# Head of a two-layer hybrid diffusion step: norm by halves, adaLN by quarters, gate tiles moved, merges split by chunks

## The chip, the cores and the metric

The kernel runs on one core of a Trainium2 chip. The metric is the device time of one launch in microseconds (us), lower is better; the time given is the median of several runs. The engines are TensorE (PE in the profile, PEld for its weight loads), VectorE (DVE), ScalarE (ACT), GpSimd (POOL) and SyncE (SP, which here only issues DMAs). Each works through its own instructions in order and waits on semaphores.

## The reference

Two layers (D = 1024 channels) run over a context of 128 tokens and a latent grid of 512 tokens, which share all weights. What matters here:

```
mod = silu(c) @ w_mod[l] + b_mod[l]              # adaLN: 6 x 1024 values, one row for context, one for latent
sh1, sc1, g1, sh2, sc2, g2 = split(mod, 6)
h = rmsnorm(x, norm1_g) * (1 + sc1) + sh1
proj = h @ w_in                                   # qkv, z, beta/alpha, hyena, fourier, three gates
merged = sigmoid(gate_a) * (y_a @ w_pa) + sigmoid(gate_b) * (y_b @ w_pb) + sigmoid(gate_c) * (y_c @ w_pc)
x = x + g1 * (merged @ w_o)
h = rmsnorm(x, norm2_g) * (1 + sc2) + sh2
x = x + g2 * ((silu(h @ w_g) * (h @ w_u)) @ w_down)
```

y_a is a chunked gated DeltaNet with scans in both directions, y_b a Hyena convolution of order 2 (its filters come from a small MLP with sines), y_c a Fourier mixing. A position table is added to the latent tokens first, and a last rmsnorm closes the trunk.

## The kernel before

Activations lie channels by tokens, as 8 tiles (k) of 128 channels by 640 tokens, worked on in two chunks (c) of 320 tokens. The products keep about fp32 accuracy with three matmuls: operands are split in a rounded hi part and a remainder lo, and out = hi*hi + hi*lo + lo*hi. `split` makes the pair: ScalarE writes hi, POOL (or VectorE) subtracts for lo. A weight of 128x1024 (512 KB) comes by SP into `wr` (two buffers) and is split into `wh` and `wl` (four buffers of 512 columns), in the order of `_stream` (line 50).

A planner written in Python (lines 360 to 495) decides at build time how the work is interleaved. Each engine has an estimated clock; the main line of `mixer` and `ffn` emits matmuls, and after every six of them calls `pump`, which lets generators in the background (`bg`) emit a step when their estimated due time has come. A step's `yield hint` says how early it may run. `finish` emits what is left of a generator at once. On the chip each engine then keeps the emitted order.

*Head* (`run`, line 2116). The filter MLP, `embed` (position table, squares of x, then `rstd`), `cond` (the conditioning vector) and `mods` for adaLN tiles 0 to 15 run as generators in the planner's order; the norm starts when `embed` and `mods` are done. `mods` (line 699) takes four tiles (a group) at a time: 32-column matmuls with the weights streaming, ScalarE copies the row, a turn through TensorE brings it into columns, VectorE adds the bias. `norm` (line 807) multiplies x by the reciprocal norm, then scales and shifts with `mod`, and splits into h. It needs sh1 (groups 0 and 4) and sc1 (groups 8 and 12). `mixer` then asks with `need` for all eight tiles of a chunk before it emits the small beta/alpha projection and the qkv projections. x is written to DRAM (`xS`) before the mixer and read back before the output projection.

*adaLN later on.* All other groups come through one tile S: each half of a group (K halves, 1024 KB) is loaded, waited for, multiplied, and only then the next half is loaded. The planner's due time grows by 4.0 us per step, beside the load's estimate. Groups 28 to 40 (layer 0) and 32 to 40 (layer 1) run beside the scans' last batch, and `self.finish(*gd, *gm)` (line 1891) closes both.

*After the scans* (line 1892 on): `delta_out` norms and gates the scans' output in the background while two tiles of gate c are projected; `finish(go)`; then the Fourier branch (`fnet`) and behind it `hyena` start in the background; four merges of branch a (two channel tiles each); four of branch c, with the gate tiles 2 to 7 between; eight gate tiles of branch b; `finish(gh)`; four merges of branch b. The last merge of a tile scales it by 0.5 and splits it, over all 640 tokens. The output projection reads the eight split tiles in order of k, chunk 0 first.

Sizes of tiles in the profile's names: `A` is a large tile, `T` 640 tokens, `U` 512 columns, `pg` and `ps` PSUM banks (three and five).

Of the kernel before, what the change touches and what calls it, by code (L numbers as in the profile page):

```python
# [18 lines left out]
P = 128  # L19
# [30 lines left out]
def _stream():  # L50
    s = [("ba", 0)] + [("in", m * P) for m in QKV_ORDER]
    s += [("in", OFF_FN + m * P) for m in range(4)]
    s += [("in", 1536 + m * P) for m in range(4)]
    s += [("in", OFF_HY + m * P) for m in range(12)]
    gate = lambda br, m: ("in", OFF_G + BR[br] * D + m * P)
    s += [gate("a", m) for m in range(8)]
    s += [gate("c", 0), gate("c", 1)]
    s += [("pa", m) for m in range(0, 8, 2)]
    s.append(("pc", 0))
    for m in range(2, 8, 2):  # L60
# [243 lines left out]
class _Net:  # L304
# [377 lines left out]
    def cond(self):  # L682

        nc = self.nc
        ct = self.kp.tile([P, 2 * KD + 30], F32, name="ct")
        nc.vector.memset(ct[:, 2 * KD:], 0.0)
        nc.sync.dma_start(ct[:, :2 * KD], self.I["cT"])
        nc.sync.dma_start(self.small, self.I["small"])
        nc.scalar.activation(ct[:, :2 * KD], ct[:, :2 * KD], AF.Silu)
        self.ct = [ct[:, 2 * k:2 * k + 32] for k in range(KD)]  # L690
# [8 lines left out]
    def mods(self, l, lo, hi, par=False, hint=0.5, first=False):  # L699

# [17 lines left out]

        def add(ps, w, h):
            for k in range(KD // 2):  # L720
                for g in range(4):
                    nc.tensor.matmul(ps[32 * g:32 * g + 32, :P], self.ct[4 * h + k], w[g][:, k * P:k * P + P],
                                     start=h + k == 0, stop=h == 1 and k == 3)

        W = {}
        if first:
            for j in range(lo, hi, 2):
                S = self.A()
                for i in range(2):
                    if j + i == hi - 4:  # L730
# [5 lines left out]
        for j in range(lo, hi, 4):  # L736
            ps = None
            for h in range(2):
                if first:
                    w = [W[j + g][:, h * 512:h * 512 + 512] for g in range(4)]  # L740
                else:
                    w = [S[:, g * 512:g * 512 + 512] for g in range(4)]
                    nc.sync.dma_start(S[:, :2048].rearrange("p (g c) -> p g c", g=4),
                                      self.I["wmod"][l, j:j + 4, :, h * 512:h * 512 + 512].rearrange("g p c -> p g c"))
# [4 lines left out]
                if first and j == lo and not h:  # L749
                    self.tables()  # L750
# [7 lines left out]
            last = j, row  # L758
        self.on(last[1])
        yield hint  # L760
        turn(*last)
# [15 lines left out]
    def rstd(self, u, n, w):  # L777

        nc = self.nc
        if u == 0:  # L780
            self.rb = []
# [3 lines left out]
        for t in range(n):  # L785
            nc.tensor.matmul(ps[:w, t:t + 1], self.ssq[:, u + t * w:u + t * w + w], self.ones[:, 0:1],
                             start=True, stop=True)
        m = self.p2.tile([P, 5], F32, tag="nm", name=self.nm("nm"))[:w, :n]
# [18 lines left out]
    def norm(self, l, gcol, sh, scl, new, place, alt=False):  # L807
# [5 lines left out]
        for s in range(2):  # L813
            v.scalar_tensor_tensor(out=a[:, s], in0=mv[:, s, scl:scl + KD], scalar=1.0,
                                   in1=par[:, gcol:gcol + KD], op0=ALU.add, op1=ALU.mult)
# [7 lines left out]
        for c in range(2):  # L823
            yield from self.wait(c)
            new(c)
            for k in range(2):
                head(k, c)
            for k in range(KD):
                t, hi, lo = q.pop(0)
                for s, u, w in (((0, 0, TP), (1, TP, NC)), ((1, 0, NC),))[c]:  # L830
                    x, g, b = t[:, u:w], a[:, s, k:k + 1], mv[:, s, sh + k:sh + k + 1]
                    if alt and k % 2:
# [3 lines left out]
                if k + 2 < KD:  # L836
# [11 lines left out]
    def norm_mod(self, l, gcol, sh, scl, alt=False):  # L848
        def new(c):
# [6 lines left out]
            y[:, c * NC:(c + 1) * NC] for y in self.h[k]]), alt)  # L856
# [61 lines left out]
    def filters(self, l):  # L918
# [30 lines left out]
        for sl in (slice(0, TS), slice(TS, T)):  # L949
# [4 lines left out]
            yield  # L954
            ps = self.ps()
# [6 lines left out]
            nc.vector.tensor_tensor(out=hs[64:, sl], in0=h2[64:, :n], in1=th[64:, :n].bitcast(F32), op=ALU.subtract)  # L962
            yield
        if not l:
            self.pre = True
# [818 lines left out]
    def merge(self, br, m, th, first, last):  # L1784
# [3 lines left out]
        for i in range(2):  # L1788
            mt = self.mg[(m + i) // 4][:, (m + i) % 4]
            for c in range(2):  # L1790
# [4 lines left out]
                if not first:  # L1795
                    nc.vector.tensor_tensor(out=mt[:, sl], in0=mt[:, sl], in1=th[i][:, sl], op=ALU.add)
                self.pump()
# [13 lines left out]
    def mixer(self, l, co):  # L1811
# [82 lines left out]
        for m in range(2):  # L1894
# [11 lines left out]
        for m in range(0, 8, 2):  # L1906
            if m:
# [3 lines left out]
            else:  # L1911
                self.finish(gf)
            self.merge("c", m, th, False, False)
# [19 lines left out]
        g = self.mod[l][:, :, 16:24]  # L1933
        self.lots(2 * (KD - O_SPLIT))
# [159 lines left out]
    def embed(self):  # L2094
# [7 lines left out]
        for k in range(KD):  # L2102
# [6 lines left out]
            if k:  # L2109
                self.sq_add(k - 1)  # L2110
            yield
        self.sq_add(KD - 1)
        yield
        yield from self.rstd(0, 5, P)

    def run(self):
# [5 lines left out]
        self.step(self.ff)  # L2122
        self.x = self.x_tile()
        n = self.bg(self.embed())
        self.step(n)
        self.cond()
        m = self.bg(self.mods(0, 0, MODS0, first=True))
        self.step(m)
        while not (n.done and m.done):
            self.finish_one([co for co in (n, m, self.ff) if not co.done])  # L2130
            if m.t > 30.0 and not self.nunit:
                self.free(0, 0)
        self.gm = self.bg(self.mods(0, MODS0, MODS1))
        self.pre = False
        self.rs, self.hn = [n, n], 0
        self.co = self.bg(self.norm_mod(0, C_G1, 0, 8, True))
        for l in range(self.depth):
            for i in range(2):
                nc.sync.dma_start(self.xS[:, 4 * i:4 * i + 4], self.xA[i])
# [100 lines left out]
```

## Time and profile before

| | |
|---|---|
| median of 3 runs | 2749.7 us (2746.98 to 2753.47) |
| the profiled execution's own time | 2748.93 us |
| its span, first to last instruction | 2747.2 us |
| TensorE busy | 2542.1 us, 93% |
| VectorE, ScalarE, POOL busy | 1784.8, 1101.5, 1272.3 us |
| mean granted TensorE clock | 0.963 |

Times in the rows are us from the span's start. A granted clock of 1.00 is 2.4 GHz, of 0.50 1.2 GHz; a stretch with both has a value between. Matmul ends are modelled, so a busy TensorE is not TensorE at its peak. A bracket behind a row says how long the engine sat idle before it and what released it. All instructions go through one helper, so they have one line number; the tiles' names tell them apart.

### The profile page before, as it was taken

The page shows a single profiled execution, that of the slowest core. Times are in us where ns is not written, and L with a number is a line of the kernel's source. Part 1 is how long each engine was busy: PE and PEld are TensorE (multiplying, and loading weights), DVE is VectorE, ACT ScalarE, POOL GpSimd, SP SyncE. Part 2 cuts the span into 40 slices and gives each one's busy share as a digit, 9 for nine tenths or more (in the row PEclk, how much of TensorE's full clock was granted, in tenths as well). Part 3 has the DMA queues.
Part 4 walks back from the last instruction along what each step waited for, and adds up shares of the span by engine and source line. Part 5 has one row for each costly group of instructions (what it writes and reads, how often), then busy time and mean ns, then how long its engine had stood idle before and what let it go on. Part 6 is the DMA issues. An engine that isn't in the chain of part 4 may idle for free. (4 is left out here: it accounts for less than half of the span.)

```text
span 2747.2 us, 55957 instructions
## 1 busy us (share of the span) xinstructions
PE 2542.1 (93%) x22520; PEld 2411.4 (88%) x22520; DVE 1784.8 (65%) x3375; ACT 1101.5 (40%) x2383; POOL 1272.3 (46%) x1228
## 2 busy tenths in 40 slices
PE   5897999979999999999988989889999999999998
PEld 3786988979999999999977779778889998999997
DVE  5467977444645686667665789665456358777775
ACT  4454464422332343333335544534223333444442
POOL 2334325332335576666632352333333365776662
PEclk8998999989999999999989999989999999999999
DMA  7442663534554235422222437425255441222222
GB/s 295 171 164 63 162 146 90 155 134 146 204 191 169 62 128 173 162 78 85 85 97 90 144 79 184 115 65 159 95 200 193 163 167 47 85 85 77 85 76 79
DMA packets 125683, 353.57 MB, mean 129 GB/s; under 512 B 11994, under 2 KB 26330, under 8 KB 118944
## 3 DMA queue, kind: packets, MB, share of 16 engines
q1 hardware_dynamic: 107856, 312.76, 34.2%
q0 software_dynamic: 17568, 37.24, 7.1%
q8 instruction: 177, 2.90, 0.4%
q14 instruction: 82, 0.67, 0.1%
HBM read 288.60 MB, written 37.24 MB: 119 GB/s over the span
## 5 line engine op out<-in xcount | busy, mean ns | idle before, releaser
L2189 PE MATMUL pg<-A,wh 128*128 128x320 f32 (+1 forms) x6304 | 1456.0, 318 | 44.3 <-POOL A L2189 10.4
L2189 PEld LDWEIGHTS pg<-A,wh 128*128 128x128 f32 (+1 forms) x6304 | 1070.5, 192 | 87.0 <-POOL A L2189 18.0
L2189 PE MATMUL pg<-A,wl 128*128 128x320 f32 (+1 forms) x3152 | 990.5, 314 | 2.3 <-DMA wl<-wr 1.8
L2189 POOL TENSOR_TENSOR wl<-wr,wh 128x512 fp32r<-128x512 f32 (+2 forms) x374 | 524.3, 1415 | 513.8 <-ACT wh L2189 486.4
L2189 PEld LDWEIGHTS pg<-A,wl 128*128 128x128 f32 (+1 forms) x3152 | 603.5, 191 | 7.1 <-DMA wl<-wr 4.2
L2189 ACT CAST wh<-wr 128x512 fp32r<-128x512 f32 (+2 forms) x486 | 287.0, 609 | 278.8 <-PE pg L2189 231.4
L2189 PE MATMUL ps<-A,wh 128*128 128x320 f32 x1696 | 378.8, 310 | 0.0
L2189 PEld LDWEIGHTS ps<-A,wh 128*128 128x128 f32 x1696 | 283.9, 188 | 1.4 <-issue 1.0
L2189 PE MATMUL ps<-A,wl 128*128 128x320 f32 x848 | 263.5, 311 | 5.0 <-POOL wl L2189 4.8
L2189 POOL TENSOR_TENSOR wl<-U,wh 128x512 fp32r<-128x512 f32 x160 | 227.8, 1441 | 43.5 <-ACT wh L2189 43.5
L2189 POOL DMA_DIRECT2D wl<-wr x112 | 98.7, 912 | 277.7 <-ACT wl L2189 264.6
L2189 PE MATMUL ps<-A,A 32*32 32x32 f32 (+5 forms) x2984 | 205.3, 239 | 9.3 <-DVE A L2189 5.5
L2189 PEld LDWEIGHTS ps<-A,A 32*32 32x32 f32 (+2 forms) x2984 | 177.3, 142 | 20.2 <-DVE A L2189 6.0
L2189 DVE TENSOR_TENSOR T<-T,T 128x320 f32<-128x320 f32 (+1 forms) x139 | 133.6, 961 | 83.7 <-ACT T L2189 79.4
L2189 POOL TENSOR_TENSOR A<-A,A 128x640 fp32r<-128x640 f32 (+5 forms) x84 | 122.2, 1473 | 121.0 <-ACT A L2189 113.1
L2189 DVE TENSOR_TENSOR A<-A 128x120 f32<-128x120 f32 (+23 forms) x690 | 161.0, 297 | 14.0 <-DMA A<-hyS 10.8
L2189 PEld LDWEIGHTS ps<-A,wl 128*128 128x128 f32 x848 | 159.7, 188 | 7.4 <-POOL wl L2189 7.3
L2189 ACT CAST wh<-U 128x512 fp32r<-128x512 f32 x160 | 99.2, 621 | 165.4 <-PE ps L2189 60.0
L2189 PE MATMUL pg<-A,A 128*128 128x320 f32 x1056 | 161.0, 310 | 0.0
L2189 PEld LDWEIGHTS pg<-A,A 128*128 128x128 f32 x1056 | 156.3, 188 | 0.7 <-issue 0.2
L2189 DVE STREAM_TRANSPOSE A<-A 32x1024 f32<-32x1024 f32 x72 | 151.2, 2120 | 1.5
L2189 DVE TENSOR_TENSOR U<-ps,U 128x512 f32<-128x512 f32 x144 | 77.9, 542 | 103.3 <-PE ps L2189 66.8
(165 smaller groups left out, 3194.7 us busy)
## 6 DMA issues: line engine op xcount, KB each, us to landing
wr<-in_wbig_dram SPq DMA_DIRECT2D x272, 512.0 KB, 3.7
A<-in_wmod_dram SPq DMA_DIRECT2D x40, 1024.0 KB, 6.4
A<-hT SPq DMA_DIRECT2D x32, 1024.0 KB, 7.7
wl<-wr POOLq DMA_DIRECT2D x112, 256.0 KB, 4.5
kSp<-U SPq DMA_DIRECT2D x40, 256.0 KB, 2.0
U<-kSp SPq DMA_DIRECT2D x40, 256.0 KB, 8.7
A<-in_wmod_dram SPq DMA_DIRECT2D x16, 512.0 KB, 10.2
hyS<-T SPq DMA_DIRECT2D x24, 320.5 KB, 3.1
```

The lines of the kernel that those rows point to most:

```text
L2189: return f(*a, **k)
```

## The change

It has four parts and some moves that belong to them.

- *Head.* The order of the generators' steps is written out by hand. adaLN groups come in the order 0, 8, 4, 12 (loads and matmuls), each turned at once. `norm` gets `halves`: channels 0 to 511 of chunk 0, then of chunk 1, then channels 512 to 1023 of each; the gain is computed per half. The first half needs groups 0 and 8 only. `embed` emits its adds and squares without yields between. `mixer` of layer 0 asks for 12 of 16 tiles before chunk 0 instead of 8. The write of x to `xS` moves behind the small projection of chunk 0. In the filter MLP both first layers come before both second ones, and its last subtraction goes from VectorE to POOL.
- *adaLN later on.* Quarters of K (512 KB) into two alternating halves of S, each load issued one step ahead of its use. The 4.0 us are added per quarter.
- *Gate c.* Four of its tiles, not two, stand between `finish(*gd, *gm)` and `finish(go)`; the merges c of tiles 0 and 2 then follow each other. The order of the weights follows.
- *Merged branches.* The split of the last merge goes per chunk of 320 tokens, for the last two tiles with VectorE; the factor 0.5 is multiplied once into the gate g1.

```diff
@@ _stream
-    s += [gate("c", 0), gate("c", 1)]
+    s += [gate("c", m) for m in range(4)]
@@ mods
+        nq = 2 if first else 4
+        w1 = D // nq
...
+            js = js[::2] + js[1::2]
...
+            todo = [(j, h) for j in range(lo, hi, 4) for h in range(nq)]
+
+            def load():
+                j, h = todo.pop(0)
+                w = S[:, h % 2 * D:h % 2 * D + D]
+                nc.sync.dma_start(w.rearrange("p (g c) -> p g c", g=4),
+                                  self.I["wmod"][l, j:j + 4, :, h * w1:h * w1 + w1].rearrange("g p c -> p g c"))
+
+            load()
+        for j in js:
             ps = None
-            for h in range(2):
+            for h in range(nq):
...
+                    w = [S[:, h % 2 * D + g * w1:h % 2 * D + g * w1 + w1] for g in range(4)]
+                    if todo:
+                        load()
                 self.on(*w, *([last[1]] if last else []))
                 if not first:
                     self.cur.t += 4.0
                 yield hint
@@ norm
-        for c in range(2):
+        for k0, c in ((k0, c) for k0 in range(0, KD, n) for c in range(2)):
             yield from self.wait(c)
-            new(c)
-            for k in range(2):
+            if k0 == 0:
+                new(c)
+            if halves and c == 0:
+                gain(k0, n)
+            for k in range(k0, k0 + 2):
                 head(k, c)
-            for k in range(KD):
+            for k in range(k0, k0 + n):
@@ merge
+                if last:
+                    hi, lo = [x[(m + i) // 4][:, (m + i) % 4][:, sl] for x in self.mgs]
+                    self.split(hi, lo, mt[:, sl], nc.vector if m == 6 else None)
                 self.pump()
-            if last:
-                hi, lo = self.mgs[0][(m + i) // 4][:, (m + i) % 4], self.mgs[1][(m + i) // 4][:, (m + i) % 4]
-                nc.vector.tensor_scalar(out=mt, in0=mt, scalar1=0.5, scalar2=None, op0=ALU.mult)
-                self.split(hi, lo, mt)
@@ mixer
-            self.need(c * KD + KD)
+            self.need(c * KD + KD if l or c else KD + KD // 2)
...
+            if c == 0:
+                for i in range(2):
+                    nc.sync.dma_start(self.xS[:, 4 * i:4 * i + 4], self.xA[i])
...
-        for m in range(2):
+        for m in range(4):
             th.append(self.Tt())
             self.gate(l, "c", m, th[m])
...
-            if m:
+            if m == 0:
+                self.finish(gf)
+            if m > 2:
                 th = [self.Tt() for _ in range(2)]
...
+        nc.vector.tensor_scalar(out=g, in0=g, scalar1=0.5, scalar2=None, op0=ALU.mult)
@@ run
+        for x in (m, cd, ff, n, ff, m, m, n, n, ff, m, m, n, *[co] * 4, m, m):
+            self.step(x)
+        self.free(0, 0)
+        for x in (*[co] * 4, ff):
+            self.step(x)
+        while not m.done:
+            self.step(m)
```

In `run`, `m` is `mods`, `cd` `cond`, `ff` the filters, `n` `embed`, `co` the norm.

## Rows read from the trace of the kernel before

**Rows 1.** The page: the span, and busy time of each engine with its share and instructions.

```profile
span 2747.2 us, 55957 instructions
...
PE 2542.1 (93%) x22520; PEld 2411.4 (88%) x22520; DVE 1784.8 (65%) x3375; ACT 1101.5 (40%) x2383; POOL 1272.3 (46%) x1228
```

**Rows 2.** Timeline of the head: start, us, engine, line, operation, tiles, [idle before].

```profile
9.92 0.69 DVE L2189 TENSOR_TENSOR A<-A,U 128x512 f32<-128x512 f32 x1 [4.96 <-DMA A<-in_xT_dram]
...
22.10 2.14 DVE L2189 SCALAR_TENSOR_TENSOR U<-U,U 128x512 f32<-128x512 f32 x3
...
31.23 12.77 SPq L2189 DMA_DIRECT2D xS<-A  x2
...
44.51 0.83 DVE L2189 TENSOR_TENSOR T<-T,T 128x640 f32<-128x640 f32 x1
...
44.69 0.59 PE L2189 MATMUL ps<-small,U 128*128 128x8 f32 x2 [4.82 <-ACT U L2189]
...
52.41 0.89 DVE L2189 TENSOR_TENSOR U<-A,ps 128x320 f32<-128x320 f32 x2 [1.43 <-PE ps L2189]
...
57.69 0.87 POOL L2189 TENSOR_TENSOR A<-U,A 128x320 fp32r<-128x320 f32 x1 [0.26 <-ACT A L2189]
...
63.00 0.46 PE L2189 MATMUL pg<-A,wh 128*128 128x320 f32 x2
...
76.86 0.33 PE L2189 MATMUL pg<-A,wh 128*32 128x320 f32 x1 [0.61 <-POOL A L2189]
```

**Rows 3.** Busy time by stretch: us, each engine, granted clock, DMA share, GB/s.

```profile
54.00:63.00 9.00, 6.90 (x24) 2.76 (x25) 8.61 (x20) 8.20 (x19) 5.47 (x7) 0.65 0.67 252
63.00:79.00 16.00, 15.39 (x129) 13.66 (x128) 4.29 (x9) 10.53 (x28) 11.34 (x11) 1.00 0.25 67
```

**Rows 4.** Timeline, scans' end of layer 0, and one row of layer 1.

```profile
539.51 1.08 PE L2189 MATMUL ps<-A,ct 128*32 128x128 f32 x32
...
549.02 1.08 PE L2189 MATMUL ps<-A,ct 128*32 128x128 f32 x32
...
550.17 9.26 SPq L2189 DMA_DIRECT2D A<-in_wmod_dram  x2
...
557.08 1.93 PE L2189 MATMUL ps<-A,ct 128*32 128x128 f32 x32 [5.00 <-DMA A<-in_wmod_dram]
...
564.10 1.94 PE L2189 MATMUL ps<-A,ct 128*32 128x128 f32 x32 [4.57 <-DMA A<-in_wmod_dram]
...
566.32 2.71 ACT L2189 ACTIVATE U<-A 128x512 f32<-128x512 f32 x5
...
582.76 3.84 DVE L2189 TENSOR_TENSOR A<-A,A 128x640 fp32r<-128x640 f32 x2 [1.42 <-ACT A L2189]
...
1916.52 1.08 PE L2189 MATMUL ps<-A,ct 128*32 128x128 f32 x32
```

**Rows 5.** Timeline, TensorE inside the merges of branch a.

```profile
602.55 0.56 PE L2189 MATMUL pg<-A,wh 128*128 128x320 f32 x2 [4.34 <-DVE A L2189]
```

**Rows 6.** Timeline, last merges to output projection, layer 0.

```profile
872.26 1.46 DVE L2189 TENSOR_SCALAR A<-A 128x640 f32<-128x640 f32 x1
...
874.53 0.41 PE L2189 MATMUL pg<-A,wh 128*128 128x320 f32 x1 [1.49 <-ACT A L2189]
...
876.15 0.63 PE L2189 MATMUL pg<-A,wh 128*128 128x320 f32 x1 [1.20 <-POOL A L2189]
```

**Rows 7.** DMA issues of the page: how many, KB each, median us to landing.

```profile
wr<-in_wbig_dram SPq DMA_DIRECT2D x272, 512.0 KB, 3.7
A<-in_wmod_dram SPq DMA_DIRECT2D x40, 1024.0 KB, 6.4
```

**Rows 8.** Timeline, 48 projection matmuls in a row, as a gate tile has.

```profile
66.53 7.19 PE L2189 MATMUL pg<-A,A 128*128 128x320 f32 x48
```

**Rows 9.** Timeline, VectorE before the last merges of layer 0.

```profile
839.73 0.49 DVE L2189 SCALAR_TENSOR_TENSOR A<-A,pg 128x320 f32<-128x320 f32 x1 [26.59 <-PE pg L2189]
```

More of the change, by code (lines that the diff above doesn't have):

```diff
@@ L56, in _stream @@
     s += [gate("a", m) for m in range(8)]
-    s += [gate("c", 0), gate("c", 1)]
+    s += [gate("c", m) for m in range(4)]
     s += [("pa", m) for m in range(0, 8, 2)]
-    s.append(("pc", 0))
-    for m in range(2, 8, 2):
+    s += [("pc", 0), ("pc", 2)]
+    for m in range(4, 8, 2):
         s += [gate("c", m), gate("c", m + 1), ("pc", m)]
@@ L687, in cond @@
         nc.sync.dma_start(ct[:, :2 * KD], self.I["cT"])
-        nc.sync.dma_start(self.small, self.I["small"])
+        self.ct = [ct[:, 2 * k:2 * k + 32] for k in range(KD)]
+        yield
         nc.scalar.activation(ct[:, :2 * KD], ct[:, :2 * KD], AF.Silu)
-        self.ct = [ct[:, 2 * k:2 * k + 32] for k in range(KD)]
     def tables(self):
@@ L757, in mods @@
             nc.scalar.copy(row, ps[:, :P])
[L758 to L761, printed above, removed]
+            if first:
+                turn(j, row)
+            else:
+                last = j, row
+        if last:
+            self.on(last[1])
+            yield hint
+            turn(*last)
     def sq_add(self, k, c=None):
@@ L787, in rstd, with spread @@
                              start=True, stop=True)
+        yield from self.spread(ps, u, n, w)
+    def spread(self, ps, u, n, w):
+        nc = self.nc
+        if u == 0:
+            self.rb = []
         m = self.p2.tile([P, 5], F32, tag="nm", name=self.nm("nm"))[:w, :n]
@@ L805, in wait, with norm @@
             yield lambda: self.rs[c].t if len(self.rs) > c and self.rs[c].done else None
-    def norm(self, l, gcol, sh, scl, new, place, alt=False):
+    def norm(self, l, gcol, sh, scl, new, place, halves=False):
         nc = self.nc
@@ L812, in norm, with gain @@
         a = self.p2.tile([P, 2, KD], F32, tag="na", name=self.nm("na"))
-        for s in range(2):
-            v.scalar_tensor_tensor(out=a[:, s], in0=mv[:, s, scl:scl + KD], scalar=1.0,
-                                   in1=par[:, gcol:gcol + KD], op0=ALU.add, op1=ALU.mult)
+        def gain(u, n):
+            for s in range(2):
+                v.scalar_tensor_tensor(out=a[:, s, u:u + n], in0=mv[:, s, scl + u:scl + u + n], scalar=1.0,
+                                       in1=par[:, gcol + u:gcol + u + n], op0=ALU.add, op1=ALU.mult)
+        if not halves:
+            gain(0, KD)
+        n = KD // 2 if halves else KD
         q = []
@@ L831, in norm @@
                     x, g, b = t[:, u:w], a[:, s, k:k + 1], mv[:, s, sh + k:sh + k + 1]
-                    if alt and k % 2:
+                    if halves and k % 2:
                         nc.scalar.activation(x, x, AF.Identity, bias=b, scale=g)
@@ L855, in norm_mod @@
         return self.norm(l, gcol, sh, scl, new, lambda k, c: (self.U()[:, :NC], *[
-            y[:, c * NC:(c + 1) * NC] for y in self.h[k]]), alt)
+            y[:, c * NC:(c + 1) * NC] for y in self.h[k]]), halves)
     def norm_blocks(self, l, gcol, sh, scl):
@@ L954, in filters @@
             yield
+        for sl in (slice(0, TS), slice(TS, T)):
+            n = sl.stop - sl.start
             ps = self.ps()
@@ L1910, in mixer @@
                     self.gate(l, "c", m + i, th[i])
-            else:
-                self.finish(gf)
-            self.merge("c", m, th, False, False)
+            self.merge("c", m, th[:2], False, False)
+            del th[:2]
         self.y["c"] = None
@@ L2122, in run @@
         self.step(self.ff)
+        cd = self.bg(self.cond())
+        self.step(cd)
         self.x = self.x_tile()
@@ L2125, in run @@
         self.step(n)
-        self.cond()
+        nc.sync.dma_start(self.small, I["small"])
         m = self.bg(self.mods(0, 0, MODS0, first=True))
[L2128 to L2132, printed above, removed]
+        self.rs, self.hn = [n, n], 0
+        co = self.co = self.bg(self.norm_mod(0, C_G1, 0, 8, True))
+        ff = self.ff
+        for x in (m, cd, ff, n, ff, m, m, n, n, ff, m, m, n, *[co] * 4, m, m):
[5 more added lines that the diff above has]
+            self.step(m)
+        assert n.done and self.hn == 8
         self.gm = self.bg(self.mods(0, MODS0, MODS1))
         self.pre = False
-        self.rs, self.hn = [n, n], 0
-        self.co = self.bg(self.norm_mod(0, C_G1, 0, 8, True))
         for l in range(self.depth):
-            for i in range(2):
-                nc.sync.dma_start(self.xS[:, 4 * i:4 * i + 4], self.xA[i])
             self.mixer(l, self.co)
```

36 lines of the change are left out of this document (15 added, 21 removed).

## The prediction

> **What bounds the kernel now.** I read the page first: TensorE is busy 2542.1 of the 2747.2 us span [rows 1]. The change removes no matmul, so what it can win is TensorE's idle time, some 200 us, and the time that TensorE spends at its lower clock after such idling. So I then listed TensorE's waits in order of time, with what ended each, and for each edit looked up the wait that it is aimed at. Four places matter.
>
> *The head.* The first 128x128 projection starts at 63.00 us [rows 2]. Until then TensorE works in scraps. VectorE adds the position table to x and sums the squares; the last sum ends at 45.34, behind it the last adaLN turn (44.69), and the first multiply of the norm comes at 52.41 [rows 2]. Lo of the norm's fourth tile is done at 58.56 [rows 2]: four tiles take 6.15 us. Between 54 and 63 us the granted clock is 0.65, a mixture of 1.2 and 2.4 GHz, and VectorE is busy 8.61 of 9.00 us; between 63 and 79 us it is 1.00 and TensorE is full [rows 3].
>
> *The end of the scans in layer 0.* Four of the six adaLN half tiles have run by 550.1. The last two each wait for their load, 5.00 and 4.57 us, in a clock that has meanwhile fallen (32 matmuls take 1.94 us in place of 1.08) [rows 4]. Their issue holds SP's queue for 9.26 us. ScalarE can only begin the scans' output at 566.32, and that output ends at 586.60 on VectorE [rows 4]. In layer 1 the last half tile ran at 1916.52 without such a wait [rows 4]: there the main stream still had matmuls left.
>
> *Inside the merges of branch a*, TensorE waits 4.34 us for VectorE, which at that moment prepares the Fourier branch and so returns no PSUM bank [rows 5].
>
> *Between the last merges and the output projection.* After the last merge VectorE scales a 128x640 tile by 0.5 (1.46 us), ScalarE rounds it, POOL subtracts; TensorE waits 1.49 and then 1.20 us [rows 6]. The same pair stands once more in layer 1 (1.47 and 1.20): two layers, one pattern.
>
> **The change part by part.** *Norm by halves (head).* The norm of channels 0 to 511 needs only the adaLN groups 0 and 8, which are now loaded and computed first; groups 4 and 12 are needed for the second half. The work does not shrink, so I follow the new hand-written order along its in-order queues, with durations of before. VectorE: one sine chain (three operations of 2.14 us in all [rows 2], with the two scalings and the clamp some 3.5), then 8 position adds of 0.69 and 7 sums of 0.83, 11.3 us, from when the first half of x lands at 9.92 [rows 2]: squares summed at about 22, not 45.3. From the last turn to the norm's first multiply before took 52.41 - 45.28 = 7.1 us. The new order puts more in front: the first group's turn behind a small sine (together 3), the second long sine on VectorE (3.5), on ScalarE its sine and two copies (1.9), and only behind those the copy and turn of group 8 (1.0). 22 + 3 + 7.1 + 3.5 + 1.9 + 1.0 = 38.5 for the first multiply, not 52.41. Then the halves stand one after the other, each behind an adaLN turn that waits for ScalarE: chunk 0 until POOL gets its fourth tile, 57.69 - 52.41 = 5.3 [rows 2]; turn 1.1; chunk 1, which has one piece per tile and not two, an estimated four fifths of that, 4.2; the small second sine with its ScalarE steps, estimated a little under the long one's, 3.2; turn and gain 1.6; that is 53.9. The second half of chunk 0 takes the same 6.15 us as four tiles before, and the matmuls behind it 0.9: the projection starts at 61.0, not 63.00. So of 14 us won at the norm's start 2.0 reach TensorE. Chunk 1 before also waited in its small projection (0.61 in the row shown [rows 2], some 0.9 over it); now it is ready long before. Sum: 2.9 us gained. Bounds: 8 gained, if the turns do not hold the halves apart; 1 lost, if the scraps keep the clock at 1.2 GHz until 64.
>
> The write of x to DRAM, which held SP from 31.23 for 12.77 us [rows 2] while it waited for the last add, goes behind the first small projection. SP is then free for weights; the same 2.6 MB move later, beside a TensorE that is full and a DMA share of 0.25 [rows 3]: nothing either way. The two hyena subtractions that go from VectorE to POOL lie where POOL has nothing to do: nothing.
>
> *adaLN by quarters.* 40 loads of 1024 KB become 80 of 512 KB into two alternating halves of the tile, each issued one step ahead; the matmuls are the same. The planner adds 4 us to a step, now per quarter. Before, a half tile came every 9.4 us (540.59 to 550.10 [rows 4]); a quarter can come no sooner than 4 us plus its 16 matmuls, and pumps are 6 matmuls, 0.9 us, apart [rows 8], so I take 5.5. From the first, near 519, seven of twelve quarters fit before the scans end at 552.08 [rows 4] and five are left, not two halves of six. A 512 KB load lands in 3.7 us where a 1024 KB one takes 6.4 [rows 7]. Two quarters are there already or on their way; behind them two pairs of load and matmuls of some 4.3 us each: the turn ends near 563, not 566.9 (564.10 + 1.94 + 0.9 for copy and turn). Gain 4 us. Layer 1, by the same pace: three of eight quarters left where one half was; the end moves from 1918.5 to about 1920.2: 1.7 us lost. Sum 2.3 gained. Bounds: 13.8 gained, if the quarters keep up and the wait goes altogether (15 us from 552 to 567, less 3.7 of work, and 2.5 for gate tiles that no longer run at 1.2 GHz); 4 lost, if two quarters more are left in each layer. The other adaLN stretches lie beside a full TensorE, with nobody waiting for their loads: nothing.
>
> A rule speaks against this edit: the Trainium skill (DMA: Bandwidth & Descriptors, Bandwidth) asks for transfers of 1 MiB or more, since each pays a fixed part; its section Anatomy of one DMA gives 2.0 us plus bytes at 436 KB/us, an estimate of 3.2 us for a quarter and 4.4 for a half. By that two quarters cost 2.0 us more than a half wherever they don't overlap; by the trace it is 2 x 3.7 - 6.4 = 1.0 [rows 7], the same direction. With 3.2 for 3.7 the two pairs above would end 1 us sooner, 3.3 us gained by this edit in place of 2.3.
>
> *Four tiles of gate c ahead of the scans' output.* A gate tile is 48 matmuls, 7.19 us [rows 8]. Two more now cover the scans' output; but that output ended at 586.60, just as the merges of branch a began, with no wait between [rows 4], so in the old order there is nothing to win. The 4.34 us inside the merges [rows 5] stay: the Fourier branch still starts behind the scans' output and lands in the same merges. What pays is the hyena branch, which loses 14.4 us of matmuls beside it. VectorE is idle for 26.59 us before 839.73, hyena being done [rows 9], so 12 us of cover remain. I take 0; bounds 3 gained (a shorter wait at the Fourier branch's end) and 4 lost (two merges in a row beside hyena's first round, both on VectorE).
>
> *Merged branches by chunks.* The 0.5 moves into the residual gate (one tiny operation for eight of 1.46 us), the rounding runs per 320 columns, the last two tiles subtract on VectorE. The output projection reaches the last tile 21 matmuls, 3.1 us, after its start, and chunk 0 of it is then complete. Both waits go: 1.49 + 1.20, in two layers 5.4 us. Bounds 6 and 2 (ScalarE's sixteen short copies for eight long ones).
>
> **Sum**: 2.9 + 2.3 + 0 + 5.4 = 10.6 us. From the profiled execution's 2748.9 (span 2747.2 and 1.7 around it; the median shown is 0.8 higher) that gives 2738.3; I say 2738.
>
> **Rivals.** *Much faster*: the quarters end with the scans and TensorE never falls to 1.2 GHz there. For it: both loads would be one step ahead. Against it: the 4 us per step. 2.9 + 13.8 + 5.4 = 22.1 us, 2727; with the head at its bound, 2722. *No change*: quarters pace worse than halves (seven left in layer 0, five in layer 1: 4 lost), the head gives 0 because TensorE enters the projection at 1.2 GHz, and the last merges give 5: about 2748. For it: the head's clock of 0.65 [rows 3], and that two loads of 512 KB take 1.0 us more than one of 1024 KB [rows 7]. The rule of the Trainium skill named above (DMA: Bandwidth & Descriptors) points to this rival. *Slower*: the hyena branch outlasts gates b. It decides from 12 us on, and each us beyond is paid in both layers; to end 5.5 us above before it must outlast by 8.1, so its 160 us must grow by some 20. For it: two merges in a row add VectorE work to its first round. Against it: later rounds lose the same work. At 10 us over, 2758. *The change doesn't do what it says*: gate c covers nothing, as costed; that is inside the forecast.
>
> **How the numbers follow.** Forecast (3 to 20 us faster) 0.54; much faster 0.22; no change 0.14; slower 0.10. A difference under 0.2% (5.5 us) is about what a measurement of this kernel cannot tell from none: above 2744.2 the forecast's small end counts as no change. Faster 0.74, same 0.17, slower 0.09. The forecast's own range is 2730 to 2745; with the much-faster case and half of the no-change case, 2720 to 2749.
>
> **What would show it.** Head: first norm multiply near 38, first 128x128 projection near 61. If the projection starts before 56, ScalarE's turns didn't hold it; if after 63, the hand-written order did. Scans' end: two waits of adaLN matmuls for loads of some 3 us each in layer 0, last turn near 563. Output projection: no wait behind the last merges. Merges of branch a: a wait of about 4 us for VectorE, still there. Gates b: VectorE idle some 12 us before the last merges; a TensorE wait there makes the prediction wrong, as does a wait for weights behind the moved write of x.

## The result, and the profile after

The changed kernel takes 2773.1 us (median of 4 runs, 2770.64 to 2776.85), the kernel before 2748.6 beside it: ratio 1.0087, 95% interval 1.0070 to 1.0105. It is some 24 us slower, where I had forecast 10 faster. The page of the changed kernel, its first rows and the adaLN loads:

```profile
span 2770.6 us, 56053 instructions
...
PE 2563.1 (93%) x22520; PEld 2418.0 (87%) x22520; DVE 1768.6 (64%) x3367; ACT 1108.2 (40%) x2400; POOL 1267.1 (46%) x1240
...
A<-in_wmod_dram SPq DMA_DIRECT2D x96, 512.0 KB, 4.3
```

Beside [rows 1]: the same 22520 matmuls, but TensorE is busy 21.0 us longer; the span is 23.4 longer. So over the whole span the loss is hardly idle time (205.1 us before, 207.5 after): the same matmuls take longer. That is a net figure: in the stretch 90 to 346 of the table below alone, TensorE's idle time grew from 27.2 to 38.4 us, and elsewhere it shrank by 8.8. The mean granted clock fell from 0.963 to 0.958; a clock is 1.00 or 0.50, so TensorE stood at 1.2 GHz for 2 x 0.037 x 2747.2 = 203 us before and 2 x 0.042 x 2770.6 = 233 after. By the trace's clock record it was busy for 154 us of the first and 180 of the second. Work takes 1.7 to 2 times as long there (in rows below, 16 adaLN matmuls 1.08 us in place of 0.64, two of 320 columns 0.90 in place of 0.46), so by an estimate 11 to 13 of the 21 us are clock.

Both kernels run the same 13268 matmuls of 320 columns, nearly all of the main line. The start of the n-th of them, after less before, tells where time went. Its change by stretch, in us, worked out so from one trace each (borders n = 192, 1152, 1824, 2112, 3264, 3744, 5664, 7392, 8256, 8736, 9888, 10368; the runs' names stand with their texts in the section on experiments):

| stretch, in time before | after | a_only | a_noX | a_head | b_only | q_steps | q_pace | b_pairs | d_only | head_d_q |
|---|---|---|---|---|---|---|---|---|---|---|
| 0-90 head | -4.5 | -5.3 | -2.7 | -3.4 | -0.1 | 0.7 | -0.5 | -0.1 | -0.1 | -3.7 |
| 90-346 first projections, filters, layer 0 | 15.0 | 14.9 | 0.9 | 0.8 | 7.6 | 14.2 | 1.5 | 1.8 | 1.4 | 0.5 |
| 346-502 scans | -1.2 | 0.2 | -0.1 | 0.4 | 1.2 | -0.4 | -0.1 | 0.3 | 0.3 | 0.4 |
| 502-592 scans' end, layer 0 | -2.5 | -1.1 | -2.1 | -2.4 | -0.5 | 1.5 | 7.0 | -5.5 | 0.1 | -10.0 |
| 592-861 merges a, c, gates b | 1.5 | 2.9 | 3.0 | -0.5 | -0.8 | -0.1 | -1.2 | -0.6 | 0.1 | -0.3 |
| 861-945 last merges, output projection | -0.6 | 3.9 | 3.9 | 1.0 | 5.0 | 1.7 | 3.8 | 1.0 | -1.7 | -2.0 |
| 945-1254 feed-forward with layer 1's adaLN | 3.9 | -1.3 | -1.3 | -1.3 | 5.7 | 3.9 | -0.1 | -1.3 | -1.3 | 0.1 |
| 1254-1619 first projections, layer 1 | 7.6 | 6.8 | 3.2 | -0.1 | -0.4 | 0.6 | 0.4 | 0.0 | -0.2 | -1.6 |
| 1619-1838 scans | 0.5 | -0.2 | 0.0 | -0.2 | -0.5 | 0.5 | 0.4 | -0.3 | -0.3 | -0.2 |
| 1838-1942 scans' end, layer 1 | 4.2 | 0.0 | 0.0 | 1.1 | 4.2 | 4.8 | 8.0 | 0.0 | 0.0 | 0.0 |
| 1942-2211 | 2.0 | 0.7 | 0.7 | -1.3 | -0.1 | -1.1 | -1.4 | 0.6 | 0.6 | -0.4 |
| 2211-2296 last merges, layer 1 | -2.7 | 2.9 | -0.1 | 0.2 | 0.3 | 0.2 | 1.6 | 2.9 | -3.2 | -2.8 |

Stretches with the same code differ by up to about 4 us from trace to trace, by where the clock falls (861 to 945 above all, where the kernel before was lucky: at the same idle time of 6 us, a_noX stood 10.3 us longer at 1.2 GHz). A difference of that size means something only where other traces repeat it. Four places lose: the first projections of both layers (15.0 and 7.6), the feed-forward stage (3.9; 5.2 beside the -1.3 of the runs in which, as in the changed kernel, the clock did not fall there), and the scans' end of layer 1 (4.2, as in b_only; 0.0 to 1.6 in the runs with the old steps at the old pace).

*Head.* The timeline: the last turn ahead of the projections, the first multiply of the norm, the first 128x128 projection.

```profile
35.49 0.89 DVE L2231 TENSOR_TENSOR U<-A,ps 128x320 f32<-128x320 f32 x2 [0.81 <-PE ps L2231]
...
51.95 0.59 PE L2231 MATMUL ps<-small,U 128*128 128x8 f32 x2 [8.34 <-ACT U L2231]
...
59.47 0.46 PE L2231 MATMUL pg<-A,wh 128*128 128x320 f32 x2
```

The norm begins at 35.49 (52.41 in [rows 2]), the projections at 59.47 (63.00): the head won 3.5 us.

*First projections, layer 0.* TensorE, VectorE and ScalarE, 100 to 131 us:

```profile
104.70 2.17 DVE L2231 SCALAR_TENSOR_TENSOR T<-T 128x80 f32<-128x80 f32 x8
...
109.82 1.22 ACT L2231 CAST A<-U 128x512 fp32r<-128x512 f32 x2 [7.52 <-DVE U L2231]
...
116.88 0.90 PE L2231 MATMUL pg<-A,wh 128*128 128x320 f32 x2 [5.86 <-ACT T L2231]
...
118.68 2.69 PE L2231 MATMUL ps<-A,A 128*128 128x512 f32 x6
...
125.04 2.89 DVE L2231 SCALAR_TENSOR_TENSOR T<-T,par,T 128x641 f32<-128x641 f32 x2 [5.14 <-ACT T L2231]
...
128.01 0.92 ACT L2231 ACTIVATE A<-T 128x256 f32<-128x256 f32 x3 [3.07 <-issue]
...
130.25 0.43 ACT L2231 ACTIVATE dex<-ps 128x160 f32<-128x160 f32 x2
...
130.60 0.94 PE L2231 MATMUL ps<-U,T 128*128 128x512 f32 x2 [4.50 <-ACT dex L2231]
```

VectorE is in the delta gates' chain of small operations (128x80). ScalarE's rounding of a filter tap (a 128x512 block of filter values) waits 7.52 us behind it, and the copies that empty projection banks (`T<-pg`) queue behind that rounding; TensorE waits 5.86 us for one. Then the gates' exponentials (`dex<-ps`) stand on ScalarE behind a silu (`A<-T`). The profile names no releaser for the 3.07 us before that silu, but it begins just as VectorE's convolution ends (125.04 + 2.89). The exponentials free a `ps` bank, and TensorE waits 4.50 us for it. The kernel before, at the same place:

```profile
112.55 1.55 PE L2189 MATMUL ps<-A,A 128*128 128x512 f32 x6
...
114.82 1.55 PE L2189 MATMUL ps<-A,A 128*128 128x512 f32 x6
...
127.77 0.43 ACT L2189 ACTIVATE dex<-ps 128x160 f32<-128x160 f32 x2
...
134.32 0.93 ACT L2189 ACTIVATE A<-T 128x256 f32<-128x256 f32 x3
```

There ScalarE waited for VectorE nearly as long (7.14 us, to 112.99), but TensorE had other matmuls to do meanwhile, twelve of the filters' transform (`ps<-A,A`) among them; in the changed kernel these come behind its wait. And the exponentials stood ahead of that silu, not behind it. So the order on TensorE and on ScalarE has changed. The two waits are 10.4 us where the kernel before has one of 4.70 (its row stands below); the rest of the 15.0 are further waits up to 280 us and 6.9 us more at 1.2 GHz, which no run takes apart.

*Feed-forward stage.* An adaLN stretch among the main line's matmuls, changed kernel:

```profile
1147.72 0.31 PE L2231 MATMUL pg<-A,wl 128*128 128x320 f32 x1
1147.96 0.64 PE L2231 MATMUL ps<-A,ct 128*32 128x128 f32 x16
1148.54 0.56 PE L2231 MATMUL pg<-A,wh 128*128 128x320 f32 x2
1148.94 0.31 PE L2231 MATMUL pg<-A,wl 128*128 128x320 f32 x1
```

and in the kernel before:

```profile
1134.63 0.31 PE L2189 MATMUL ps<-A,wl 128*128 128x320 f32 x1
...
1135.07 0.31 PE L2189 MATMUL ps<-A,wl 128*128 128x320 f32 x1
1135.31 1.08 PE L2189 MATMUL ps<-A,ct 128*32 128x128 f32 x32
1136.32 0.56 PE L2189 MATMUL ps<-A,wh 128*128 128x320 f32 x2
1136.72 0.31 PE L2189 MATMUL ps<-A,wl 128*128 128x320 f32 x1
```

From one `wl` matmul to the next is 0.44 us; with 32 adaLN matmuls between, 1.65; with 16, 1.22. So 32 cost 1.21 us and twice 16 cost 1.56: each further stretch costs 0.35 us. The stage has 16 such stretches before and 32 after.

*Scans' ends, and behind them.* The last adaLN quarters of layer 0 and of layer 1; inside the merges of branch a; VectorE ahead of the last merges:

```profile
561.67 0.64 PE L2231 MATMUL ps<-A,ct 128*32 128x128 f32 x16 [0.91 <-DMA A<-in_wmod_dram]
565.28 1.08 PE L2231 MATMUL ps<-A,ct 128*32 128x128 f32 x16 [2.96 <-DMA A<-in_wmod_dram]
...
569.87 1.08 PE L2231 MATMUL ps<-A,ct 128*32 128x128 f32 x16 [1.97 <-DMA A<-in_wmod_dram]
...
572.13 1.08 PE L2231 MATMUL ps<-A,ct 128*32 128x128 f32 x16 [1.18 <-DMA A<-in_wmod_dram]
...
624.64 0.87 PE L2231 MATMUL pg<-A,wh 128*128 128x320 f32 x2 [3.86 <-DVE A L2231]
...
848.10 0.49 DVE L2231 SCALAR_TENSOR_TENSOR A<-A,pg 128x320 f32<-128x320 f32 x1 [12.50 <-PE pg L2231]
...
1940.01 0.71 PE L2231 MATMUL ps<-A,ct 128*32 128x128 f32 x16 [2.98 <-DMA A<-in_wmod_dram]
```

*Last merges to output projection*, busy time by stretch in both layers (the places of [rows 6]):

```profile
868.00:888.00 20.00, 20.00 (x171) 18.82 (x171) 10.98 (x21) 6.67 (x13) 9.60 (x9) 1.00 0.67 254
2236.00:2256.00 20.00, 20.00 (x171) 18.82 (x170) 10.83 (x21) 5.82 (x12) 9.60 (x9) 1.00 0.62 223
```

TensorE is busy for all of the 20 us: both waits have gone.

### The profile page after: what moved, and what is told of

The parts are those of the page before. It is cut to its first block, busy times and chain, and to the rows that moved or that the text cites. A ratio compares the mean times of both kernels' runs of the same rounds, so it can differ in the third digit from the quotient of the medians.

```text
span 2770.6 us, 56053 instructions
## 1 busy us (share of the span) xinstructions
PE 2563.1 (93%) x22520; PEld 2418.0 (87%) x22520; DVE 1768.6 (64%) x3367; ACT 1108.2 (40%) x2400; POOL 1267.1 (46%) x1240
## 5 line engine op out<-in xcount | busy, mean ns | idle before, releaser
L2231 POOL TENSOR_TENSOR A<-A,A 128x320 fp32r<-128x320 f32 (+5 forms) x92 | 119.4, 1314 | 118.7 <-ACT A L2231 109.3
L2231 DVE SCALAR_TENSOR_TENSOR T<-T,par,T 128x641 f32<-128x641 f32 x84 | 108.6, 1293 | 77.7 <-POOL T L2231 29.3
```

The source lines that it names most:

```text
L2231: return f(*a, **k)
```

## Experiments

Each is an edit of the kernel before, or of the changed one where it says so; where no diff is shown, it is made of parts of the diffs that are. Ratios are to the kernel before, with the 95% interval.

**The four parts alone** (a_only the head's part, b_only the quarters, c_only gate c, d_only the merges). Theory 1: the head's part changed the order around the filters. Theory 2: the quarters.

> Only the head's part on the kernel before: the order of the first steps written out, the norm by halves, the filters' two first layers ahead of both second ones, the write of x behind the first gemm of the mixer. Theory 1 (the loss between 90 and 297 us of layer 0, +16 us, and between 1400 and 1660 us of layer 1, +7.5 us, comes from the new order around the filters): 2762 to 2772 us. Theory 2 (the quarters of the adaLN weights are to blame for nearly all of it): 2744 to 2748 us, as my sum for this part alone (-2.9).

> Only the adaLN tiles by quarters, loaded one step ahead. Theory 1: 2750 to 2757 us: it loses the 5 us seen between 1153 and 1265 us in the feed-forward stage of layer 0 and what the scans' end of layer 1 lost, and gains some 2 to 4 at the scans' end of layer 0. Theory 2: 2765 to 2772 us, since the quarters that lie among the first projections and the filters push those apart.

> Only the four tiles of gate c ahead of the scans' output, and merges c 0 and 2 together. Both theories: within 3 us of the kernel before (2746 to 2751 us); the stages from gates a to the end of gates b took 1.7 us longer in layer 0 and about 1 us in layer 1 of the changed kernel.

> Only the split of the last merges by chunks with the factor folded into g1. Both theories: the two waits of 1.49 and 1.20 us ahead of the output projection go in each layer, 2738 to 2745 us (my sum: -5.4). If the 2.7 us that the stretch behind the output projection lost in layer 0 (and 1.5 in layer 1) belong to this part: 2743 to 2747 us.

Measured: head's part 2773.2 us (1.0079, 1.0056 to 1.0103); quarters 2770.8 (1.0072, 1.0049 to 1.0095); gate c 2754.1 (1.0011, 0.9999 to 1.0023); merges 2744.0 (0.9969, 0.9957 to 0.9981). Gate c came 3 us above its figure. Both theories fell as rivals: each of the first two parts loses nearly the whole alone, and in the table both lose in the stretch 90 to 346 (14.9 and 7.6), the quarters elsewhere too. The sum of the four would be +39; together they lose 24. By the traces some 8 of these 15 us lie in the stretch 90 to 346, where the four alone add up to 23.4 and lose 15.0 together: a stall that is there already is not paid twice. The rest is mainly at the last merges of both layers, where the first three stood longer at 1.2 GHz than the kernel before (by 10, 10 and 7 us in the stretch 861 to 945). The quarters alone, timeline of the three engines there:

```profile
127.11 2.79 DVE L2203 SCALAR_TENSOR_TENSOR T<-T,par,T 128x641 f32<-128x641 f32 x2 [5.13 <-POOL wl L2203]
...
129.98 0.92 ACT L2203 ACTIVATE A<-T 128x256 f32<-128x256 f32 x3 [2.98 <-issue]
...
132.22 0.43 ACT L2203 ACTIVATE dex<-ps 128x160 f32<-128x160 f32 x2
...
132.57 1.51 PE L2203 MATMUL ps<-U,T 128*128 128x512 f32 x2 [10.80 <-ACT dex L2203]
```

On ScalarE the same order as in the changed kernel, and here one wait of 10.80 us. In the kernel before, TensorE's row at this place:

```profile
126.51 1.51 PE L2189 MATMUL ps<-U,T 128*128 128x512 f32 x2 [4.70 <-ACT U L2189]
```

**What in the head's part.** Filters' order alone (f_only), and the head without it and without the moved write of x (a_head):

```diff
             self.sin_mlp(ps[:64, :n], 64, fq[:64], bb[:64, 0:1], h1[:64, sl], n)
             yield
+        for sl in (slice(0, TS), slice(TS, T)):
+            n = sl.stop - sl.start
             ps = self.ps()
...
-            nc.vector.tensor_tensor(out=hs[64:, sl], in0=h2[64:, :n], in1=th[64:, :n].bitcast(F32), op=ALU.subtract)
+            nc.gpsimd.tensor_tensor(out=hs[64:, sl], in0=h2[64:, :n], in1=th[64:, :n].bitcast(F32), op=ALU.subtract)
```

> Only the order of the filters on the kernel before: both first layers ahead of both second ones, and the lo of the hidden layer subtracted on POOL. Theory 1a (the new order of the filters' steps is what cost layer 1's 7 us between 1411 and 1608 us of the run of the head's part alone, and a part of layer 0's): 2756 to 2763 us. Theory 1b (the filters are innocent, the shifted head is what counts): 2749 to 2752 us.

> The head's part without the new order of the filters and without the move of the write of x: only the written-out order of the first steps, the norm by halves, the groups' order. Theory 1a: the start won in the head (5 us at 85 us) is kept for the most part, 2744 to 2752 us. Theory 1b: the projections that start earlier meet the filters, the delta gates and the table loads in another order and stall, 2758 to 2770 us.

Measured: filters 2753.1 (1.0005, 0.9994 to 1.0017); head without both 2745.0 (0.9975, 0.9961 to 0.9989). Theory 1a's figure held for the head; for the filters neither's did, and alone they lose nothing that counts. Then the write alone (x_only; moved behind the first gemm of `mixer`), and the head's part without it (a_noX):

```diff
             ps = self.gemm(W[-1], self.h, c, M=32, free=((1, 0), (0, 1))[c])
+            if c == 0:
+                for i in range(2):
+                    nc.sync.dma_start(self.xS[:, 4 * i:4 * i + 4], self.xA[i])
```

> Only the write of x behind the first gemm of the mixer, on the kernel before. Theory 5a (the moved write is what the head's part lost by): 2757 to 2770 us. Theory 5b (the new order of the filters loses it, once the head is shorter: their steps meet the delta gates' chain of small operations on VectorE): 2748 to 2753 us.

> The head's part whole but for the move of the write of x. Theory 5a: 2744 to 2752 us. Theory 5b: 2762 to 2774 us, with a TensorE wait of 8 to 10 us near 100 us in layer 0 as in the head's part alone, and some 5 us lost in layer 1 between 1440 and 1510 us.

Measured: write alone 2755.3 (1.0016, 1.0006 to 1.0025); head's part without it 2748.1 (0.9991, 0.9979 to 1.0003). Theory 5a's figure held for the second, neither's for the first: no piece alone loses over 5 us, but the write on top of the earlier head and the filters' order turns -2 into +22 us, 14 of it in the stretch 90 to 346. What the write changed there, on VectorE; first the head's part whole (a_only), with the row of TensorE that waits:

```profile
101.70 0.68 DVE L2221 TENSOR_TENSOR U<-U,A 1x512 f32<-1x512 f32 x1 [7.96 <-DMA A<-in_fb_dram]
102.30 0.18 DVE L2221 TENSOR_SCALAR T<-T 128x80 f32<-128x80 f32 x1
...
105.07 2.18 DVE L2221 SCALAR_TENSOR_TENSOR T<-T 128x80 f32<-128x80 f32 x8
...
109.53 0.69 DVE L2221 TENSOR_TENSOR U<-ps,A 128x512 f32<-128x512 f32 x1
...
110.27 1.52 PE L2221 MATMUL ps<-U,T 128*128 128x512 f32 x2 [9.72 <-DVE U L2221]
```

and without the write:

```profile
100.21 0.68 DVE L2220 TENSOR_TENSOR U<-U,A 1x512 f32<-1x512 f32 x1 [2.67 <-DMA A<-in_fb_dram]
100.82 0.67 DVE L2220 TENSOR_TENSOR U<-ps,A 128x512 f32<-128x512 f32 x1
...
105.50 2.18 DVE L2220 SCALAR_TENSOR_TENSOR T<-T 128x80 f32<-128x80 f32 x8
```

The gates' chain (102.30 to 109.5) came ahead of the second tap's eviction, VectorE's read that empties its PSUM bank (109.53, not 100.82), so TensorE waited 9.72 us for a bank. That is a different order. But VectorE also waited longer for the load of the filters' bias (7.96 us, not 2.67), so a later transfer is a rival. The kernel with the gates' second step held until five taps are out (a_gates) tests both:

```diff
+        if not l:
+            yield lambda: 0.0 if self.tapped else None
```

> The head's part alone, with one wait more in the issue order: in layer 0 the delta gates' second step (the chain of small operations, 7 us on VectorE) is issued only behind the filters' first five taps. Theory 6 (order: with the gates' chain ahead of the second tap's eviction, TensorE waited 9.72 us for a PSUM bank): that wait shrinks to under 3 us and the kernel takes 2758 to 2768 us, 5 to 14 less than the head's part alone (2773). Rival (the loss is from the write of x itself, 2.6 MB among the loads at 47 to 65 us): the time stays at 2768 to 2776 us.

Measured: 2762.1 (1.0037, 1.0024 to 1.0049), and TensorE's rows there:

```profile
106.19 1.51 PE L2224 MATMUL ps<-U,T 128*128 128x512 f32 x2 [4.08 <-DVE U L2224]
133.63 1.05 PE L2224 MATMUL ps<-dsel,small 128*64 128x20 f32 x16 [9.02 <-ACT U L2224]
```

The wait shrank from 9.72 to 4.08, less than expected, and another of 9.02 appeared where the gates now run. From 90 to 346 the loss fell from 14.9 to 2.7, though VectorE's wait for the bias was longer still (9.55 us): so the order, not the later load, made most of that loss. But the scans then lost 9.1, with 10.3 us more at 1.2 GHz than in the kernel before; the profiled execution, of 2769.2 us, was the slowest of its ten, so a part of that is this execution's own. The time is within the theory's figure, and the theory holds in kind: order alone moved some 10 us about; holding one step back is no cure.

**What in the quarters.** One number (the planner's allowance, q_pace), then the number of steps with the old loads (q_steps):

```diff
-                    self.cur.t += 4.0
+                    self.cur.t += 8.0
```

> The kernel before with one number changed: the planner's allowance per half adaLN tile is 8.0 us in place of 4.0, as two quarters of 4.0 have. Loads, matmuls and their number of steps are those of before, only the order in which the planner issues them shifts. Theory 3 (pace and order cost what the quarters lost at the first projections of layer 0, +7, and at the scans' end of layer 1, +8 and -4): 2757 to 2764 us, and the feed-forward stage of layer 0 as long as before. Rival (the number of loads and steps is what costs): 2749 to 2753 us.

```diff
-                add(ps, w, h)
+                add(ps, w, h, range(2))
+                self.on(*w)
+                yield hint
+                add(ps, w, h, range(2, 4))
```

> The kernel before with each half adaLN tile's 32 matmuls in two steps of 16, at the old pace and with the old loads of 1024 KB. Theory 4 (each time TensorE goes to the 32-column matmuls and back it pays some 0.33 us, whatever the loads): the feed-forward stage of layer 0, from the 4032nd to the 5664th 320-column matmul, 5 us longer as with the quarters, and the whole 2756 to 2765 us. Rival (the loads of 512 KB with runs of 1 KB are to blame): that stage unchanged, 2749 to 2753 us.

Measured: pace 2769.7 (1.0063, 1.0046 to 1.0080); steps 2774.3 (1.0078, 1.0063 to 1.0093). Pace costs 7.0 and 8.0 us at the two scans' ends, more than expected, and 1.5 in the first projections, where I had expected 7. Steps cost 3.9 in the feed-forward stage (5.2 more than in a_only or d_only), as expected, but 14.2 in the first projections, so the whole missed its figure by 9: half-size steps alone flip the order there (in their trace, too, the gates' chain stands on VectorE ahead of the second tap's eviction). Next the quarters at 2.0 us each (b_fast), and the old steps with each load cut in two (b_pairs):

```diff
-                    self.cur.t += 4.0
+                    self.cur.t += 2.0
```

> The adaLN quarters alone with the planner's allowance of 2.0 us per quarter, so 4.0 per half as before. Theory 3 (pace): the scans' ends no longer lose, 2752 to 2760 us; what stays are the 40 further stretches of 0.33 us, of them 5 us in the feed-forward stage of layer 0. Rival (quarters lose the same at any pace, by their number and their loads): 2766 to 2775 us.

```diff
-                    nc.sync.dma_start(S[:, :2048].rearrange("p (g c) -> p g c", g=4),
-                                      self.I["wmod"][l, j:j + 4, :, h * 512:h * 512 + 512].rearrange("g p c -> p g c"))
+                    for i in range(2):
+                        nc.sync.dma_start(S[:, :2048].rearrange("p (g c) -> p g c", g=4)[:, :, i * 256:i * 256 + 256],
+                                          self.I["wmod"][l, j:j + 4, :, h * 512 + i * 256:h * 512 + i * 256 + 256].rearrange("g p c -> p g c"))
```

> The kernel before with each adaLN half loaded in two transfers of 512 KB with runs of 1 KB, back to back, waited for together; the matmuls stand in steps of 32 at the old pace. Theory 4 (what costs is the number of TensorE stretches and the order, not the size of the loads): 2747 to 2754 us, feed-forward stage as before; at the scans' end of layer 0 at most 2 us more. Rival (the 512 KB loads): 2755 to 2765 us.

Measured: fast quarters 2768.6 (1.0071, 1.0053 to 1.0090); loads cut in two 2746.4 (0.9988, 0.9971 to 1.0005). For the quarters the rival's figure held. The smaller loads cost nothing, and at the end of layer 0's scans they pay 5.5 us, as TensorE begins on the first part; I had expected the two parts to be waited for together:

```profile
555.76 0.64 PE L2190 MATMUL ps<-A,ct 128*32 128x128 f32 x16 [1.57 <-DMA A<-in_wmod_dram]
557.09 0.65 PE L2190 MATMUL ps<-A,ct 128*32 128x128 f32 x16 [0.69 <-DMA A<-in_wmod_dram]
```

The quarters at 2.0 us win 11.5 us there, but lose 13.0 in the first projections, 4.7 in the feed-forward stage and 4.2 at the scans' end of layer 1, where no quarter waits for its load any more: theory 3 was right for the scans' end of layer 0 alone.

**Versions made of what pays** (head_d; head_d_q with the quarters at one place; head_cd_q with gate c too).

> The head's part without the filters' order and the write of x, together with the last merges by chunks. If what these two gained alone adds up (-5.6 and -6.8): 2736 to 2741 us. If one shifts the order of what the other meets: 2743 to 2750 us.

> The head's part without filters' order and write of x, the last merges by chunks, and the quarters at 2.0 us each for the three groups at the end of layer 0's scans alone. Theory: the 13.7 us that this place won in the quarters at 2.0 us come on top of the 2739 of the two other parts, less some 3 us for six more stretches: 2726 to 2732 us. Rival (the scans themselves are then stretched by the quarters among them, or the order flips elsewhere): 2736 to 2745 us.

```diff
-        gm = [self.bg(self.when_met(self.dpr, self.mods(l, (MODS1, MODS2)[l], 40)))]
+        gm = [self.bg(self.when_met(self.dpr, self.mods(l, (MODS1, MODS2)[l], 40, fine=not l)))]
```

> The fast version (head without filters' order and write of x, last merges by chunks, quarters at 2.0 us for the end of layer 0's scans alone) with the four tiles of gate c ahead of the scans' output as well. My forecast's term for gate c (nothing; bounds 3 gained, 4 lost): 2732 to 2739 us. If the cover now is needed, since the quarters end with the scans and the scans' output is the next to be late: 2726 to 2731 us.

Measured: head and merges 2739.3 (0.9959, 0.9949 to 0.9970); with the quarters at the one place 2735.3 (0.9932, 0.9912 to 0.9951); with gate c as well 2731.2 (0.9932, 0.9917 to 0.9947). The first two add up as expected; the 10.0 us at the one place stand in the table (2.0 of them also in head_d, without the quarters), though the median fell by 4 only, between the two figures. The last two beat the kernel before by 0.7%; gate c adds nothing to the ratio, and its median too fell between the two figures. The last quarters of layer 0 in the second of the three, with no wait and at full clock:

```profile
546.58 0.64 PE L2232 MATMUL ps<-A,ct 128*32 128x128 f32 x16
549.78 0.64 PE L2232 MATMUL ps<-A,ct 128*32 128x128 f32 x16
553.19 0.64 PE L2232 MATMUL ps<-A,ct 128*32 128x128 f32 x16
```

**The causes inside the changed kernel.** Halves again (after_halves); and the write of x where it was (after_noX):

> The changed kernel with the adaLN tiles by halves again, as in the kernel before; all else stays. Sum of the parts run alone: head's part +22, gate c +3 to 0, last merges -7: 2764 to 2770 us. If the quarters carry what is lost behind the first projections of layer 0 (5 in the feed-forward stage, 1 at each of the merges of branch b, 4 to 6 at the scans' end of layer 1, less 2 to 4 won at that of layer 0): 2758 to 2764 us.

> The changed kernel with the write of x where it was before; all else stays. If the moved write alone set off the loss in the first projections of layer 0: 2756 to 2763 us. If the quarters there set off the same loss by themselves, as the quarters alone did (a TensorE wait of 10.8 us behind the delta gates' exponentials): 2764 to 2772 us.

Measured: 2761.3 (1.0041, 1.0026 to 1.0056) and 2765.9 (1.0062, 1.0045 to 1.0078). Each second figure held. Taking out the quarters gives back 12 us, taking out the moved write 7. In the stretch 90 to 346 they still lose 14.8 and 11.8: either trigger is enough for that stall. The quarters' own loss stands elsewhere (feed-forward, scans' end of layer 1), the write's in layer 1's first projections (1.7 without it, 7.6 with).

## Why the prediction was wrong

*Head: right where it was worked out, wrong behind it.* I forecast the first multiply near 38 and the projection near 61; they came at 35.49 and 59.47, and the head kept most of it when left alone (0.9975). The steps that failed are the two moves beside it: the write of x, which I costed at "nothing either way", and the filters, where I costed the subtractions at "nothing" and gave the new order of the layers no term at all. I looked for what hides a transfer, and not at the fact that the planner decides the order of all that follows from its due times. On top of the earlier head they cost 28 us (2745.0 to 2773.2): 14 of them in the stretch 90 to 346, by the order shown above, and some 7 in layer 1's first projections, where no run shows the mechanism. That the write acts through the planner's count of transfers fits the code, but was not tried by itself.

*adaLN by quarters: the failed step is "The other adaLN stretches lie beside a full TensorE, with nobody waiting for their loads: nothing."* A full TensorE is just where a further stretch costs: 0.35 us each, 16 of them in the feed-forward stage, 5.6 by the rows and 5.2 measured. The Trainium skill (TensorEngine Tiling (Array Packing), Key Properties) says that a change of the tiling mode drains TensorE; the 0.35 us agree in direction, though no run shows what in a switch costs them. The rest is order again (first projections) and the scans' end of layer 1: I forecast 1.7 lost, 4.2 were. In the changed kernel the last quarter waited 2.98 us there and the clock fell; but at 2.0 us each the quarters lost the same 4.2 without that wait, so its cause stays open. At layer 0's scans I forecast 4 won. The changed kernel won 2.5 there, but with halves again it won 1.5 too, and the quarters alone won 0.5: so they gave 0.5 to 1.0, with four waits of 0.91 to 2.96 us for my two of 3. My bound of 13.8 for quarters that keep up was not passed: at 2.0 us the place won 11.5 and 10.0 (8.0 beside head_d).

*The rule on 1 MiB* (the Trainium skill, DMA: Bandwidth & Descriptors, Bandwidth) that I weighed against this edit did not decide: loads of 512 KB in place of 1024 KB gave 0.9988 (0.9971 to 1.0005), and the measurement stands. My estimates of 3.2 and 4.4 us went by the same page's section Anatomy of one DMA, where the Trainium skill gives that fit for DMAs that GpSimd issues; these loads are issued by SP. The run also puts my price from the trace right: two loads of 512 KB in place of one of 1024 KB did not cost the 1.0 us that I took.

*Gate c: right.* Nothing (1.0011, and the same ratio with and without it in the fast version); the wait inside the merges of branch a stayed (3.86), VectorE idled 12.50 us before the last merges where I had said 12.

*Merges by chunks: right.* Both waits went in both layers; 6.8 us by the medians for my 5.4.

*The sum.* Of my terms, 2.9 gained by the head came out as 22 lost (5.6 gained without the two moves), 2.3 gained by the quarters as 20 lost, 0 for gate c as 0 to 3 lost, and 5.4 gained by the merges as 6.8.

*Rivals.* The slower case came, but not by its mechanism: the hyena branch did not outlast gates b, and its 2758 is far from 2773. Missing among the rivals was the one that came: that an edit in one place changes the order which a planner makes for all that follows.

## What to carry to other kernels

Where a planner or a scheduler at build time sets the order, an edit that moves a step, a load or an estimate is an edit of everything behind it: compare the order of each engine's queue before and after, above all around shared banks, before costing the edit at nothing. Splitting background work into finer steps pays only where its consumer waits; beside a full engine every further switch is paid. Try parts one by one and keep those that pay: here the head, the merges and the quarters at one place gave 0.7%, all parts together lost 0.9%.

## What the runs showed of the hardware

At 2.4 GHz a stretch of 32-column matmuls among 128-column ones cost TensorE 0.35 us beyond its matmuls (1.21 us for 32, 0.78 for 16). One 1024 KB load cut into two of 512 KB was no slower and let the consumer begin sooner (5.5 us at one place).
